# Three transformer blocks, mixture of experts at the end: the last two experts' results are summed on chip instead of in DRAM

## The chip, the cores and the metric

The kernel runs on one core of a Trainium2 chip, in one launch. The metric is the device time of a launch in microseconds (us). TensorE (PE) does the matmuls, VectorE (DVE), ScalarE (ACT) and GpSimd (POOL) the rest; SP and POOL issue the DMAs.

## The reference, cut to what matters

Three blocks follow each other on a sequence of 512 tokens of 1024 features. Only the end of the third is touched by the change:

```
x  = layer_norm(ALPHA * x + xa, ln2_g, ln2_b)
ff = hierarchical_moe(x, ...)          # each token goes to 2 of 32 experts
x  = layer_norm(ALPHA * x + ff, ln3_g, ln3_b)
```

An expert computes `(silu(x Wg) * (x Wu)) Wd`, with Wg and Wu of 1024 by 512 and Wd of 512 by 1024; a token's result is the sum of its two experts' outputs, each times a routing weight. The weights of one expert are 6.3 MB in float32. Products are made accurate by splitting each factor into a high and a low part (`H` and `L`) that TensorE takes in its one-pass float32 format (fp32r).

## The kernel before, in words

Routing sorts the 32 experts by the number of their tokens. Three experts come first by number ("fixed", `N_FIX`), so that their weights can be loaded before the routing is known; columns 18 to 31 (`N_BIG` on) hold the experts with the fewest tokens. Those are "small": at most 64 tokens, whose high and low parts stand side by side in the 128 columns of one operand, so that each step takes two matmuls instead of three; in exchange the two halves are added by 16 `fold` matmuls (L2137). A big expert takes 48 matmuls of 512 columns for gate and up and 24 for down; a small one 32 and 16.

The list `cols` (L2179) gives the order: five big experts, then small and big in turn, and a small one (column 31) as the last. The experts lie in a pipeline written out by hand: the block under `tc.manual_schedule` (L2203) fixes the order on PE, ACT, DVE, POOL and SP. In step `i` PE does the first half of the gate product of expert `i+1`, the transposes (or folds) of expert `i` (`mid`), the rest of the gate, `down` of `i`, and `up` of `i+1`; in step 30 `up` comes before `down`. The weights come in 12 pieces of 512 KB per expert, issued by SP (L1839); ACT casts each to its high part (L189) and DVE subtracts to get the low part (L190), up to five pieces ahead of PE, in five pairs of buffers.

`gather` (L2079) fetches an expert's tokens from `x2d`, the DRAM copy of the normalized residual that `resid_ln` spills at L415. `down` ends with two ACT evictions of PSUM times the routing weight (L2151) and an indirect DMA from POOL that adds the rows to `zd` in DRAM (L2152). `zd` has two halves of 512 rows; the second takes the low halves of small experts. Both are zeroed by eight DMAs (L1321) in the source of block 3, which depend on constants alone.

After the experts `K.x` (slot "X") is loaded from `x2d` (L2231). Then comes a loop over overflow experts (L2236) with a trip count read from the routing; in this trace its body does not run, but each engine reads the count, waits for the others' semaphores and for the DMA queues, and branches. Then eight DMAs from POOL add both halves of `zd` to the four tiles of `K.x` (L2255), two for a tile, and the last layer norm goes tile by tile: statistics on DVE for tile 0 and on ACT for the others, a power on POOL (L197), two DVE passes (L2266, L2267) and a store (L2268). Outside the manual block a planner places the instructions by its costs; so SP issues the zero fills at the kernel's start and the load of L2231 early in the expert stage.

Of the kernel before, what the change touches and what calls it, by code (L numbers as in the profile page):

```python
# [8 lines left out]
F32 = mybir.dt.float32  # L9
F32R = mybir.dt.float32r  # L10
I32 = mybir.dt.int32
AF = mybir.ActivationFunctionType
# [4 lines left out]
P = 128  # L17
S = 512
# [63 lines left out]
class K:  # L82
# [305 lines left out]
    def resid_ln(self, w, act, nk, xd, g, b, slots, zslot="A", spill=None, korder=None, after=None, mid=None):  # L388
        nc = self.nc
        g_, b_ = self.brow(g), self.brow(b)  # L390
        zt = self.slot(zslot, [P, 4, D])
        def reload():
            if xd is not None:
                for t in range(4):
                    nc.sync.dma_start(self.x[:, t], xd[t])
            if mid:
                mid[1]()

        if xd is not None:
            self.new_x()  # L400
        x = self.x
        hT = {}
        st = self.small([P, 4, 2, 6])

        def fn(half):
            def f(t, ps):
                hs = slice(half * 512, half * 512 + 512)
                nc.vector.scalar_tensor_tensor(zt[:, t, hs], x[:, t, hs], ALPHA, ps, ALU.mult, ALU.add)
                nc.vector.bn_stats(st[:, t, half], zt[:, t, hs])
                if half:  # L410
                    if not hT and slots:
                        hT[0] = self.hTn = self.new_hT(*slots)
                    self.layer_norm(x[:, t], zt[:, t], g_, b_, st[:, t])
                    if spill is not None:
                        nc.sync.dma_start(spill[t * P:(t + 1) * P], x[:, t])  # L415
                    if after:
                        after(t)
                    else:
                        self.to_hT(x[:, t], t, *hT[0], ps="t")
            return f  # L420

        for half in range(2):
            self.lin_b(w, half * 512, 512, act, fn(half), nk=nk, korder=korder, tail=3 * half,
                       mid=None if half else (mid[0] if mid else 0, reload))
# [881 lines left out]
def block3(K, out):  # L1306
# [10 lines left out]
    kd, vd = K.dram([P, 8, 256]), K.dram([P, 2, 512])  # L1317

    zd = K.dram([2 * S, D])
    for t in range(8):  # L1320
        nc.sync.dma_start(zd[t * P:(t + 1) * P].rearrange("p (a b) -> p a b", a=4),  # L1321
                          K.cst[:, C_CAUS - 384:C_CAUS - 128].unsqueeze(1).to_broadcast([P, 4, 256]))
    K.psum(f="f", nO="D", nS="B", nT="C", g="A")
# [552 lines left out]
        nc.tensor.transpose(ps[:, P:P + 36], lT[:, t % 2], K.ident[:36, :36])  # L1876
        tt(lg[:, t], ps[:, P:P + 36], bias, ALU.add)

    K.resid_ln(A("xa_wo"), K.actf((oH, oL)), 8, None, A("ln2_g"), A("ln2_b"), None, spill=x2d, after=logits)
    while K.bg:  # L1880
        K.bg.pop(0)()
    eslot = []
# [21 lines left out]
    with ExitStack() as ctx:  # L1904
# [166 lines left out]
        class Expert:  # L2071
            def __init__(self, i, c, small=False):
                self.i, self.small = i, small
                self.it, self.ws = (itok[:, c:c + 1], wsl[:, c:c + 1]) if isinstance(c, int) else c
                self.n = 64 if small else P

            def gather(self):
# [62 lines left out]
                tt(hT, sg, pt[:, 256:512], ALU.mult)  # L2140
                K.split(self.dH[:, :, 0:64], self.dH[:, :, 64:128], hT.rearrange("p (k t) -> p k t", k=4))

            def down(self, parts):
                yt = yt2[self.i % 2]
                pss = [K.psc() for _ in range(2)]
                for k in range(4):
                    h, l = parts()
                    for half, ps in enumerate(pss):
                        self.step(ps, self.dH, self.dL, k, 4, h[:, half], l[:, half])
                for half, ps in enumerate(pss):  # L2150
                    nc.scalar.activation(yt[:, half * 512:half * 512 + 512], ps, AF.Copy, scale=self.ws)  # L2151
                nc.gpsimd.indirect_dma_start(out=zd, out_offset=bass.IndirectOffsetOnAxis(ap=self.it, axis=0),  # L2152
                                             in_=yt, in_offset=None, bounds_check=2 * S - 1, oob_is_err=False, compute_op=ALU.add)


        class Feed:
# [10 lines left out]
        def ln3():  # L2167
            rows = brow(), brow()
            for dst, n in zip(rows, ("ln3_g", "ln3_b")):
                nc.sync.dma_start(dst[0:1], A(n).rearrange("(o d) -> o d", o=1))  # L2170
                for half in range(2):
                    hs = slice(half * 512, half * 512 + 512)
                    ps = K.psf()
                    mm(ps, K.cst[0:1, C_TRIU:C_TRIU + P], dst[0:1, hs], start=True, stop=True)
                    nc.scalar.copy(dst[:, hs], ps)
            return rows


        cols = [*range(N_FIX + 2), *(c for i in range(13) for c in (N_BIG + i, N_FIX + 2 + i)), 31]  # L2179

        def psrc(c):
            if c < N_FIX:
# [20 lines left out]
        with tc.manual_schedule(engines={getattr(mybir.EngineType, n) for n in ORDERED}):  # L2203
            for i in range(3):
                E[i].gather()
                if i < 2:
                    E[i].xT()
            E[0].gate1(feed)
            E[0].gate2(feed)
            E[0].up(feed)  # L2210
            for i, ex in enumerate(E):
                n1 = E[i + 1] if i < 31 else None
                if i == 8:
                    g_, b_ = ln3()
                if n1:
                    n1.gate1(feed)
                ex.mid()
                if n1:
                    n1.gate2(feed)
                if i < 30:  # L2220
                    E[i + 2].xT()
                if i < 29:
                    E[i + 3].gather()
                if i == 30:
                    n1.up(feed)
                ex.down(feed)
                if i < 30:
                    n1.up(feed)
        K.new_x()
        for t in range(4):  # L2230
            nc.sync.dma_start(K.x[:, t], x2d[t * P:(t + 1) * P])  # L2231

        it1 = rp.tile([P, 1], I32)
        ws1 = rp.tile([P, 1], F32)
        nx = nc.values_load(eidi[0:1, 7:8], min_val=0, max_val=7)
        with tc.For_i(0, nx, 1) as i:  # L2236
            ev = nc.values_load(eidi[0:1, bass.ds(i, 1)], min_val=0, max_val=31)
            nc.vector.tensor_copy(it1, itok[:, 32:39][:, bass.ds(i, 1)])
            nc.vector.tensor_copy(ws1, wsl[:, 32:39][:, bass.ds(i, 1)])
            src = [w[bass.ds(ev, 1)].rearrange("o r n -> (o r) n") for w in (wG, wU, wD)]  # L2240
            ex, parts = Expert(0, (it1, ws1)), Feed([lambda p=p: eload(p) for p in epieces(*src)])
            ex.gather()
            ex.xT()
            ex.gate1(parts)
            ex.gate2(parts)
            ex.up(parts)
            ex.mid()
            ex.down(parts)

        jt = K.slot("hH", [P, 4, D])  # L2250
        mu = rp.tile([P, 4, 4], F32)
        st = rp.tile([P, 2, 6], F32)
        for t in range(4):
            for z in (zd[t * P:(t + 1) * P], zd[S + t * P:S + (t + 1) * P]):
                nc.gpsimd.dma_start(K.x[:, t], z, accum_op=ALU.add)  # L2255
        for t in range(4):
            z, j, m_ = K.x[:, t], jt[:, t], mu[:, t]
            if t == 0:
# [51 lines left out]
```

## Time and profile before

| what | value |
|---|---|
| median of 3 runs | 2969.16 us (2954.52 to 2970.5) |
| profiled execution | 2949.98 us, of which 2.1 us lie outside its span |
| PE busy | 2815.3 us (95%) |
| DVE, ACT, POOL busy | 1731.2, 1391.1, 181.9 us |
| last expert matmul ends | 2901.9 us |
| end of the span | 2947.9 us |

All times from a view are counted from the span's start. A PE matmul's listed duration is longer than the distance to the next one, as matmuls are pipelined; the distance is its price. The mean number of bytes in flight says little: the expert stage (from about 2340 us) moves some 370 GB/s, the rest far less. A DMA's row on POOL or SP is its issue; the transfer itself ends later, at its landing.

### The profile page before, as it was taken

The page shows a single profiled execution, that of the slowest core. Times are in us where ns is not written, and L with a number is a line of the kernel's source. Part 1 is how long each engine was busy: PE and PEld are TensorE (multiplying, and loading weights), DVE is VectorE, ACT ScalarE, POOL GpSimd, SP SyncE. Part 2 cuts the span into 40 slices and gives each one's busy share as a digit, 9 for nine tenths or more (in the row PEclk, how much of TensorE's full clock was granted, in tenths as well). Part 3 has the DMA queues.
Part 4 walks back from the last instruction along what each step waited for, and adds up shares of the span by engine and source line. Part 5 has one row for each costly group of instructions (what it writes and reads, how often), then busy time and mean ns, then how long its engine had stood idle before and what let it go on. Part 6 is the DMA issues. An engine that isn't in the chain of part 4 may idle for free. (4 is left out here: it accounts for less than half of the span.)

```text
span 2947.9 us, 38804 instructions
## 1 busy us (share of the span) xinstructions
PE 2815.3 (95%) x14484; PEld 2339.1 (79%) x14484; DVE 1731.2 (59%) x2827; ACT 1391.1 (47%) x2325; POOL 181.9 (6%) x149
## 2 busy tenths in 40 slices
PE   8999999999999999999999999999999699999993
PEld 7788878888878878778888889787877588888882
DVE  4543453434576666755333362766564798998994
ACT  4432333332345445532222223756333388888883
POOL 0000000000000000000000000000000111221112
PEclk9999999999999989999999999999999799999996
DMA  6233333333331222133333344111432699999994
GB/s 205 86 93 93 100 93 95 98 99 94 119 86 47 68 61 58 47 121 100 95 100 93 100 137 124 36 37 56 164 121 108 217 351 384 381 375 377 384 376 89
DMA packets 332488, 432.76 MB, mean 147 GB/s; under 512 B 33583, under 2 KB 242154, under 8 KB 332298
## 3 DMA queue, kind: packets, MB, share of 16 engines
q1 hardware_dynamic: 322826, 417.52, 42.2%
q0 software_dynamic: 9472, 12.74, 2.0%
q8 instruction: 114, 1.87, 0.3%
q14 instruction: 76, 0.62, 0.1%
HBM read 419.04 MB, written 32.51 MB: 153 GB/s over the span
## 5 line engine op out<-in xcount | busy, mean ns | idle before, releaser
L164 DVE TENSOR_TENSOR wl<-raw,wh 128x1024 fp32r<-128x1024 f32 (+2 forms) x322 | 391.0, 1214 | 681.2 <-ACT wh L163 678.0
L163 ACT CAST wh<-raw 128x1024 fp32r<-128x1024 f32 (+2 forms) x322 | 336.4, 1045 | 862.2 <-PE pf L272 368.0
L272 PE MATMUL pf<-hL,wh 128*128 128x512 f32 x1272 | 502.0, 395 | 0.0
L272 PE MATMUL pf<-hH,wh 128*128 128x512 f32 x1208 | 477.9, 396 | 0.0
L272 PE MATMUL pf<-hH,wl 128*128 128x512 f32 x1208 | 475.8, 394 | 0.0
L272 PEld LDWEIGHTS pf<-hL,wh 128*128 128x128 f32 x1272 | 239.6, 188 | 50.5 <-issue 3.1
L272 PEld LDWEIGHTS pf<-hH,wh 128*128 128x128 f32 x1208 | 227.5, 188 | 52.5 <-issue 4.6
L272 PEld LDWEIGHTS pf<-hH,wl 128*128 128x128 f32 x1208 | 227.2, 188 | 48.7 <-issue 2.6
L190 DVE TENSOR_TENSOR wl<-ew,wh 128x1024 fp32r<-128x1024 f32 x186 | 216.9, 1218 | 6.2 <-ACT wh L189 5.5
L2098 PE MATMUL pc<-wh,hL 128*128 128x512 f32 x512 | 204.0, 398 | 0.0
L2099 PE MATMUL pc<-wl,hL 128*128 128x512 f32 x512 | 200.8, 392 | 0.0
L197 POOL TENSOR_TENSOR s<-s,mhalf 128x1 f32<-128x1 f32 (+1 forms) x69 | 57.9, 839 | 2234.4 <-DVE s L195 2228.8
L189 ACT CAST wh<-ew 128x1024 fp32r<-128x1024 f32 x186 | 184.4, 1056 | 8.4 <-PE pc L316 4.6
L347 PE MATMUL pf<-wh,hH 128*128 128x256 f32 (+2 forms) x576 | 163.9, 285 | 0.0
L314 PE MATMUL pc<-wh,B 128*128 128x512 f32 x416 | 163.1, 392 | 0.0
L315 PE MATMUL pc<-wl,B 128*128 128x512 f32 x416 | 162.8, 391 | 0.0
L348 PE MATMUL pf<-wl,hH 128*128 128x256 f32 (+2 forms) x576 | 162.6, 282 | 0.0
L349 PE MATMUL pf<-wh,hL 128*128 128x256 f32 (+2 forms) x576 | 162.0, 282 | 0.0
L316 PE MATMUL pc<-wh,C 128*128 128x512 f32 x320 | 124.6, 389 | 0.0
L2101 PE MATMUL pc<-wh,hL 128*128 128x512 f32 x288 | 113.7, 395 | 0.0
L2098 PEld LDWEIGHTS pc<-wh,hL 128*128 128x128 f32 x512 | 97.4, 190 | 19.9 <-issue 0.8
L2099 PEld LDWEIGHTS pc<-wl,hL 128*128 128x128 f32 x512 | 97.1, 190 | 19.5
(718 smaller groups left out, 5851.9 us busy)
## 6 DMA issues: line engine op xcount, KB each, us to landing
raw<-w_in SPq DMA_DIRECT2D x111, 512.0 KB, 4.0
raw<-w_ff SPq DMA_DIRECT2D x64, 512.0 KB, 3.9
ew<-moe_w_down SPq DMA_DIRECT2D x64, 512.0 KB, 12.5
B<-moe_w_gate SPq DMA_DIRECT2D x64, 512.0 KB, 7.2
hH<-moe_w_up SPq DMA_DIRECT2D x64, 512.0 KB, 11.4
A<-moe_w_down SPq DMA_DIRECT2D x64, 512.0 KB, 9.7
ew<-moe_w_up SPq DMA_DIRECT2D x62, 512.0 KB, 10.0
ew<-moe_w_gate SPq DMA_DIRECT2D x60, 512.0 KB, 10.3
```

The lines of the kernel that those rows point to most:

```text
L163: nc.scalar.copy(h, raw)
L164: nc.vector.tensor_sub(l, raw, h)
L189: self.nc.scalar.copy(h, src)
L190: self.nc.vector.tensor_sub(l, src, h)
L272: self.nc.tensor.matmul(ps[:n, sl], u[:, k], v[:, sl], start=(k == 0 and i == 0 and sl.start == 0), stop=(k == nk - 1 and i == 2), skip_gr ...
L314: mm(pss[t][:, :n], ah[:, ts], wh[:, k], start=(kg == 0), stop=False)
L315: mm(pss[t][:, :n], ah[:, ts], wl[:, k], start=False, stop=False)
L347: mm(o[t], ah[:, ts], wh[:, k], start=st, stop=False, skip_group_check=True)
L348: mm(o[t], ah[:, ts], wl[:, k], start=False, stop=False, skip_group_check=True)
L349: mm(o[t], al[:, ts], wh[:, k], start=False, stop=(kg == nk - 1), skip_group_check=True)
L2098: mm(ps, aH[:, k], h, start=(k == 0), stop=False)
L2099: mm(ps, aH[:, k], l, start=False, stop=(self.small and k == n - 1))
```

## The change: what it does, and the diff

The results of the last two experts in the list no longer go to DRAM. `down(keep=True)` splits them, times the routing weight, into a high part (ACT) and a low part (DVE), written into the expert's own, no longer needed, input buffers; and it builds four one-hot matrices per expert on DVE, slot against token of a tile, from the table of token numbers. `combine` multiplies them: for each tile and half 4 matmuls into a PSUM bank, and a DVE addition to `K.x`. To that end both last experts are big ones: `cols` starts with three big experts, alternates from there, and ends with two big ones.

The first half of `zd` starts as the residual (`resid_ln` spills each tile twice) instead of zeros, so four zero fills and the load of `x2d` at the end go. The eight loads of `zd`, four plain and four adding, are issued by POOL at the start of step 30, inside the manual order; an overflow expert, in the loop, goes by `combine` as well.

```diff
-                    if spill is not None:
-                        nc.sync.dma_start(spill[t * P:(t + 1) * P], x[:, t])
+                    for d in spill or ():
+                        nc.sync.dma_start(d[t * P:(t + 1) * P], x[:, t])
...
-    for t in range(8):
+    for t in range(4, 8):
...
-    K.resid_ln(..., spill=x2d, after=logits)
+    K.resid_ln(..., spill=(x2d, zd), after=logits)
...
+                if keep:
+                    self.yH, self.yL = (fl(v) for v in xh2[self.i % 2])
+                    self.oh = K.raw.tile([P, 4, P], F32R, name=K.nm("oh"), tag="raw")
+                    for t in range(4):
+                        ts_(self.oh[:, t], cc(G_I128, P), t * P + 1.0, self.tk, ALU.add, ALU.is_equal)
+                    for half, ps in enumerate(pss):
+                        hs = slice(half * 512, half * 512 + 512)
+                        nc.scalar.activation(self.yH[:, hs], ps, AF.Copy, scale=self.ws)
+                        stt(self.yL[:, hs], ps, self.ws, self.yH[:, hs], ALU.mult, ALU.subtract)
+                    return
...
+        def combine(*es):
+            for t in range(4):
+                for half in range(2):
+                    hs = slice(half * 512, half * 512 + 512)
+                    ps = K.psc()
+                    todo = [(e.oh[:, t], y[:, hs]) for e in es for y in (e.yH, e.yL)]
+                    for i, (o, y) in enumerate(todo):
+                        mm(ps, o, y, start=(i == 0), stop=(i == len(todo) - 1))
+                    tt(K.x[:, t, hs], K.x[:, t, hs], ps, ALU.add)
...
-        cols = [*range(N_FIX + 2), *(c for i in range(13) for c in (N_BIG + i, N_FIX + 2 + i)), 31]
+        cols = [*range(N_FIX), *(c for i in range(14) for c in (N_BIG + i, N_FIX + i)), N_BIG - 1]
...
+                if i == 30:
+                    K.new_x()
+                    for z in (0, S):
+                        for t in range(4):
+                            nc.gpsimd.dma_start(K.x[:, t], zd[z + t * P:z + (t + 1) * P],
+                                                **({"accum_op": ALU.add} if z else {}))
...
-                ex.down(feed)
+                ex.down(feed, i > 29)
...
-        K.new_x()
-        for t in range(4):
-            nc.sync.dma_start(K.x[:, t], x2d[t * P:(t + 1) * P])
+            combine(E[30], E[31])
...
-            ex.down(parts)
+            ex.down(parts, True)
+            combine(ex)
...
-        for t in range(4):
-            for z in (zd[t * P:(t + 1) * P], zd[S + t * P:S + (t + 1) * P]):
-                nc.gpsimd.dma_start(K.x[:, t], z, accum_op=ALU.add)
```

## Rows read from the trace of the kernel before

**Rows 1.** The page's first line: span and instructions.
```profile
span 2947.9 us, 38804 instructions
```

**Rows 2.** Chain that ended last, its longest piece: start us, us, what.
```profile
2919.26 11.03 DMA X<-dr
```

**Rows 3.** Timeline 2880 to 2950: start, us, engine line op, [idle before <-releaser].
```profile
2890.88 3.81 PEld L2137 LDWEIGHTS pt<-fold,scr 128*128 128x128 f32 x16
...
2896.65 0.80 PE L2098 MATMUL pc<-wh,dHL 128*128 128x512 f32 x1 [1.82 <-DVE dHL L190]
...
2901.31 0.40 PE L2098 MATMUL pc<-wh,dHL 128*128 128x512 f32 x1
...
2901.51 1.27 ACT L2151 ACTIVATE C<-pc,wsl 128x512 f32<-128x512 f32 x2 [5.37 <-PE pc L2099]
2901.54 0.40 PE L2099 MATMUL pc<-wl,dHL 128*128 128x512 f32 x1
2903.05 1.56 POOL L2152 DMA_INDIRECT dr<-C,itok  x1 [7.96 <-ACTq L2236]
2907.76 2.75 POOL L2255 DMA_DIRECT2D X<-dr  x3 [3.16 <-issue]
...
2922.58 1.28 DVE L2260 BATCH_NORM_STATS2 st<-X 128x6 f32<-128x512 f32 x2 [25.98 <-DMA X<-dr]
...
2927.26 15.52 SPq L2268 DMA_DIRECT2D out<-X  x4
...
2929.64 1.28 DVE L2267 SCALAR_TENSOR_TENSOR X<-X,s,bc 128x1024 f32<-128x1024 f32 x1 [0.44 <-POOL s L197]
...
2932.64 1.28 DVE L2267 SCALAR_TENSOR_TENSOR X<-X,s,bc 128x1024 f32<-128x1024 f32 x1 [0.46 <-POOL s L197]
2936.90 1.06 ACT L2263 ACTIVATE hH<-X 128x1024 f32<-128x1024 f32 x1 [6.62 <-DMA X<-dr]
```

**Rows 4.** Windows of 20 us: length, busy us PE PEld DVE ACT POOL, clock, DMA.
```profile
2820.00:2840.00 20.00, 20.00 (x93) 17.30 (x93) 17.09 (x19) 16.62 (x24) 4.51 (x3) 1.00 0.97 368
```

**Rows 5.** Waits 2320 to 2900: us in total, times, longest.
```profile
PEld pc L2099 <- DVE wl L190: 0.2, 1, 0.2
```

**Rows 6.** Timeline of DVE, single instructions of the routing and the expert stage.
```profile
2310.91 0.29 DVE L1951 TENSOR_TENSOR C<-C,mv 128x128 f32<-128x128 f32 x1
...
2374.72 0.68 DVE L2124 TENSOR_TENSOR scr<-scr,pc 128x512 f32<-128x512 f32 x1
...
2392.49 0.68 DVE L2124 TENSOR_TENSOR scr<-scr,pc 128x512 f32<-128x512 f32 x1
...
2844.40 0.68 DVE L2124 TENSOR_TENSOR scr<-scr,pc 128x512 f32<-128x512 f32 x1
...
2878.76 0.68 DVE L2124 TENSOR_TENSOR scr<-scr,pc 128x512 f32<-128x512 f32 x1
...
2889.03 4.62 DVE L190 TENSOR_TENSOR wl<-A,wh 128x1024 fp32r<-128x1024 f32 x4
```

**Rows 7.** Windows of 1 us in the last expert's down product, columns as above.
```profile
2898.00:2899.00 1.00, 1.00 (x4) 0.71 (x4) 0.00 (x0) 0.00 (x0) 0.00 (x0) 0.50 0.00 0
```

**Rows 8.** Timeline of POOL: the scatter of the third last expert.
```profile
2873.52 1.83 POOL L2152 DMA_INDIRECT dr<-C,itok  x1 [16.11 <-ACT C L2151]
```

**Rows 9.** The scatters' line L2152: durations of the issue in ns, landing.
```profile
L2152 POOL DMA_INDIRECT dr<-C,itok x32: 1553/1848/2343, 2370.0 to 2903.0; - x32
...
DMA to landing us min/median/max: 2.7/8.2/10.9
```

**Rows 10.** DMA issues 2840 to 2950: count, size, median us to landing.
```profile
X<-dr POOLq DMA_DIRECT2D x8, 512.0 KB, 9.0
```

**Rows 11.** Timeline of SP: zero fills, the reload of X, the last weights.
```profile
32.12 9.63 SPq L1321 DMA_DIRECT2D dr<-cst  x8
...
2374.83 1.80 SPq L2231 DMA_DIRECT2D X<-dr  x4
...
2864.97 4.08 SPq L1839 DMA_DIRECT2D A<-moe_w_down  x4
```

More of the change, by code (lines that the diff above doesn't have):

```diff
@@ L1877, in logits @@
         tt(lg[:, t], ps[:, P:P + 36], bias, ALU.add)
-    K.resid_ln(A("xa_wo"), K.actf((oH, oL)), 8, None, A("ln2_g"), A("ln2_b"), None, spill=x2d, after=logits)
+    K.resid_ln(A("xa_wo"), K.actf((oH, oL)), 8, None, A("ln2_g"), A("ln2_b"), None, spill=(x2d, zd), after=logits)
     while K.bg:
@@ L2073, in __init__ @@
                 self.i, self.small = i, small
-                self.it, self.ws = (itok[:, c:c + 1], wsl[:, c:c + 1]) if isinstance(c, int) else c
+                self.it, self.ws, self.tk = [v[:, c:c + 1] for v in (itok, wsl, tab)] if isinstance(c, int) else c
                 self.n = 64 if small else P
@@ L2141, in mid, with down @@
                 K.split(self.dH[:, :, 0:64], self.dH[:, :, 64:128], hT.rearrange("p (k t) -> p k t", k=4))
-            def down(self, parts):
+            def down(self, parts, keep=False):
                 yt = yt2[self.i % 2]
@@ L2225, in block3 @@
                     n1.up(feed)
-                ex.down(feed)
+                ex.down(feed, i > 29)
                 if i < 30:
                     n1.up(feed)
-        K.new_x()
-        for t in range(4):
-            nc.sync.dma_start(K.x[:, t], x2d[t * P:(t + 1) * P])
+            combine(E[30], E[31])
         it1 = rp.tile([P, 1], I32)
         ws1 = rp.tile([P, 1], F32)
+        tk1 = rp.tile([P, 1], F32)
         nx = nc.values_load(eidi[0:1, 7:8], min_val=0, max_val=7)
@@ L2239, in block3 @@
             nc.vector.tensor_copy(ws1, wsl[:, 32:39][:, bass.ds(i, 1)])
+            nc.vector.tensor_copy(tk1, tab[:, 32:39][:, bass.ds(i, 1)])
             src = [w[bass.ds(ev, 1)].rearrange("o r n -> (o r) n") for w in (wG, wU, wD)]
-            ex, parts = Expert(0, (it1, ws1)), Feed([lambda p=p: eload(p) for p in epieces(*src)])
+            ex, parts = Expert(0, (it1, ws1, tk1)), Feed([lambda p=p: eload(p) for p in epieces(*src)])
             ex.gather()
```

## The prediction

> **What bounds the kernel now.** I read the page first: the profiled span is 2947.9 us [rows 1]; the whole execution, 2949.98, is 2.1 more, and the median of the runs shown, 2969.16, lies 19.2 above it. Then the chain that ended last: its largest piece is not an engine but a transfer, X<-dr, with a link of 11.03 us [rows 2]. The timeline of the last 70 us shows why. The last expert matmul starts at 2901.54 and lasts 0.40, so PE is done at 2901.94, 46.0 us before the end. In these 46 us come the scatter (2903.05), the loop's code, eight loads (from 2907.76), and a layer norm that starts at 2922.58 and waits for loads between its tiles: the last tile gets going at 2936.90, and the last store is issued at 2927.26 + 15.52 = 2942.78 [rows 3].
>
> Before that the expert stage is PE's: 20.00 of 20 us busy at full clock, while the DMA engines are busy 0.97 of the time at 368 GB/s [rows 4]. Both are nearly full, but the weights are in time: all that PE waited for them is 0.2 us [rows 5]. So what is taken from DMA there gains nothing in this trace, and what is taken from PE gains all.
>
> **The change part by part.**
>
> *The order of experts.* Place 3 gets a small expert for a big one, place 31 a big one for a small one; the 30 others stay. A big expert lasts 17.8 us (2374.72 to 2392.49), a pair 34.4 (2844.40 to 2878.76), so a small one 16.6 [rows 6]. Place 3 thus takes 1.2 us off everything behind it. Place 31 needs 48 matmuls for gate and up instead of 32; at a distance of 0.23 us (2901.31 to 2901.54) that adds 16 x 0.23 = 3.7 [rows 3].
>
> *The end of the last expert.* Before, it runs from the folds' start at 2890.88 to 2901.94, 11.1 us, with an idle gap of 1.82 before `down` [rows 3]; after that gap the granted clock in 2898 to 2899 is 0.50, the lower level of 1.2 GHz [rows 7]. Now there are no folds, but DVE is late: behind the last weight split stand four one-hot compares of 128x128 at 0.29 each (nearest row, same size, another operation), two low parts at 0.68 from PSUM, and only then the low part of the new `hd` at 0.68 [rows 6]. That last split goes into a buffer that PE frees six matmuls before the end of `down` of place 30 (1.4 us); a subtraction takes 4.62 / 4 = 1.2 [rows 6], the cast before it about as much (estimate from that), so it ends 1.0 behind `down`. 1.0 + 1.2 + 1.4 + 0.7 = 4.3 us. PE can use 0.45 of that for two matmuls. From there 22 matmuls take 22 x 0.23 = 5.1, and about 1.2 more if the clock falls after the wait, as it did before; together 10.2, in place of 11.1. Bounds: 8 us if DVE interleaves the compares, 13 if all 24 run at half clock. PE's end: 2901.94 - 1.2 + 3.7 - 0.9 = 2903.5.
>
> *The combine.* 32 matmuls of 512 columns in fp32r, the form of L2098. For the first bank place 30's two run at once; place 31's last low part comes 1.6 us after PE's end (two ACT evictions at 0.64, two DVE ones at 0.68 behind the first [rows 3, 6]), and then six banks of 4 x 0.23 follow: 1.9 + 5.5 = 7.4. DVE adds each bank in 0.68, less than the 0.92 that PE takes for one, so only the last shows: 8.2 us. Bounds: 7.9, and 15 if PE stays at the lower level. The waits are short, so I take 8.2.
>
> *The loads of zd.* Eight issues on POOL behind the scatter of place 29. POOL has nothing else to do then but the loop's code, and the powers of the layer norm. That scatter is issued at 2873.52 [rows 8], now 1.2 earlier, and lands after 8.2 (2.7 to 10.9) [rows 9]: 2880.5. The eight lasted 2936.90 - 2907.76 = 29.1 us before, with adding loads that wait for their tile's first one, 9.0 each in the median [rows 3, 10]; the same now gives 2909.6. The four plain ones now go first and side by side, so I take 25: 2905.5. The last tile's additions are due at 2903.5 + 6.7 = 2910.2. Hidden, with 0.6 to 5 us to spare; each microsecond beyond costs one. The last weights are issued at 2864.97 to 2869 [rows 11], so these loads do not push them back.
>
> By the Trainium skill (SBUF — State Buffer, "SBUF: two separate sides") a DMA from POOL can stand still while VectorE holds the port that both share, since POOL writes the descriptors; its box speaks of a DMA that waits until the VectorE operation's end. Here DVE splits weights all the time, and the scatters' issues take 1.85 us in the median and at most 2.34, against 1.56 at 2903.05 with DVE idle [rows 3, 9]: a delay of 0.3 to 0.8, not a split's whole 1.22. By the rule in full, 8 x 1.2 = 9.6 us would move the landing to 2915 and cost 5; by the rows, 8 x 0.3 = 2.4 stays hidden.
>
> *The loop.* It now stands between the additions and the layer norm. Before, POOL needed 3.16 us from its last issue's end to its first load, with its code, its waits and a first fetch behind the branch [rows 3]; that is the nearest row for DVE. I take 3.1 (1 to 5). What used to hide it is gone: the other engines were waiting for loads.
>
> *The layer norm.* The same instructions, but all tiles are there at once: tile 0 takes 2922.58 to 2927.26 = 4.7 from statistics to store, a further tile 3.0 (2929.64 to 2932.64) [rows 3], together 13.7. ACT's statistics run ahead, as they wait for no load. 11.9 if the planner fills DVE's wait for the power with the next tile. From the end of the last store's issue, 2942.78, to the span's end it was 5.1; with the issue itself, some 0.35, 5.5, and that stays.
>
> *What goes or moves at no price.* The reload of X ran on SP at 2374.83 [rows 11], in the stage where PE had its weights: hidden, 0. Four of eight zero fills, 1.2 us of SP's queue each at 32 to 41 us [rows 11], while PE has work: 0 (to -2). The four extra spills follow one of the same tile on the same queue; at worst they push the preloads of the first experts' weights back by 2 MB at 368 GB/s = 5.7 us [rows 4]; PE did not wait for weights, so 0, or 2 if the first gather gets in behind them.
>
> **Sum.** PE ends at 2903.5; + 8.2 + 3.1 + 13.7 + 5.5 = 2934.0, against 2947.9: 13.9 us less, 2936 in place of 2949.98. Applied to the median, 2969.16 - 13.9 = 2955.3. Of the 46.0 us behind PE's end 30.5 stay, and 1.6 of the gain is paid back by the big expert in last place.
>
> **The rivals.**
>
> *The loads are late.* They land behind 2910, at 29 us or more and slow issues, or PE stays at half clock in the combine (7 us). For it: the margin is 0.6 at the upper bound, and the landing of the scatter alone varies by 8. Against: eight were served in 29 with the layer norm's waits between them. Price 5 to 9, so 2962.
>
> *They do not overlap at all (slower).* If something holds POOL's loads until place 31 is done (a wait on slot X, on `zd`, or behind the loop's preparations), they start at 2903.5 and end 29 later, at 2932.6, where the layer norm no longer runs between them: + 1.4 for the last additions + 3.1 + 13.7 + 5.5 = 2956.3, 8 more than before; with four adding loads one after the other (11 + 4 x 9.0 = 47) it is 2974, 26 more. The middle is +17, 2986. It decides from a landing after 2924. For it: before, the adding loads waited for the plain ones. Against: slot X is free early, as the reload of before was issued into it at 2374.83 [rows 11].
>
> *More than the tail.* The runs 20 us above the profiled execution may be such in which weights come late. There the missing 2 MB reload, 5.7 us at 368 GB/s [rows 4], would count, and DVE's filled waits add 1.8: 21 less, 2948. Against: nothing here shows such a run.
>
> **How the numbers follow.** Runs of this kernel tell some 0.5%, 14.8 us, from no change, and the forecast is just short of it. Chances: forecast 0.64, split by its own bounds into 0.31 beyond 14.8 us and 0.33 within; late loads 0.14, within; no overlap 0.10, of it 0.08 slower; more than the tail 0.12, faster. Faster 0.43, same 0.49, slower 0.08. The range: the terms' bounds are -6 and +9, and the runs of one kernel spread by 16 to 20, with the profiled execution at the bottom: down to 2932 (2936 and some), up to 2967 (late loads and a little more).
>
> **What would show it.** Right: PE's last expert matmul at 2901 to 2906; a combine of some 8 us with PE at clock 1.00; the last X<-dr landing before its tile's addition; DVE's first statistics about 3 us behind the last addition; tiles 3.0 apart. The chain would name PE and DVE, not X<-dr. Wrong: an addition that waits for DMA, a PE wait for weights in the expert stage, a clock of 0.50 through the combine, or a join that takes over 5 us because each engine fetches code behind the branch.

## The result, and the profile after

The changed kernel takes 2942.95 us in the median of 20 runs (2933.41 to 2963.12), the kernel before 2963.27 over 20 runs beside them (2951.92 to 2970.52). The ratio is 0.9944, 95% interval 0.9928 to 0.9961: 16.6 us less, 11.6 to 21.3 (the two medians differ by 20.3). One execution of the kernel before, beside the last runs below, took 5023 us at a clock of 0.729; it counts in no ratio and no median. The forecast was 2955.3, 13.9 less than the median of the three runs known then.

The two profiled spans hide this at first: 2947.9 us before [rows 1], 2946.2 after. The first row that tells why is the first expert's gate and up, long before anything the change touches. Timeline of DVE, the first such eviction, before and then after:

```profile
2357.68 0.68 DVE L2124 TENSOR_TENSOR scr<-scr,pc 128x512 f32<-128x512 f32 x1
```

```profile
2371.65 0.68 DVE L2124 TENSOR_TENSOR scr<-scr,pc 128x512 f32<-128x512 f32 x1
```

The profiled execution after is 14.0 us late already. Windows (length, busy us of PE, PEld, DVE, ACT, POOL, granted clock, DMA) of the second block of the network, before:

```profile
1150.00:1170.00 20.00, 18.46 (x137) 16.09 (x137) 10.01 (x22) 11.26 (x25) 0.00 (x0) 1.00 0.32 93
1170.00:1183.00 13.00, 12.54 (x78) 10.06 (x77) 10.52 (x32) 8.13 (x20) 0.00 (x0) 1.00 0.00 1
1250.00:1272.00 22.00, 20.13 (x124) 15.98 (x123) 17.92 (x54) 16.57 (x49) 3.15 (x5) 1.00 0.00 1
```

and after:

```profile
1150.00:1170.00 20.00, 18.45 (x134) 15.78 (x133) 10.14 (x22) 11.39 (x25) 0.00 (x0) 0.98 0.32 93
1170.00:1183.00 13.00, 13.00 (x48) 10.22 (x48) 6.71 (x21) 6.81 (x17) 0.00 (x0) 0.51 0.00 1
1250.00:1272.00 22.00, 21.76 (x80) 16.80 (x79) 13.47 (x38) 12.47 (x30) 0.00 (x0) 0.53 0.03 13
```

PE was just as busy ahead of it (18.46 and 18.45 of 20 us), and then it runs at the lower level, 1.2 GHz, in one execution and not in the other: 48 matmuls instead of 78 in the same 13 us. That is chance between executions, not the change: in another execution of the changed kernel (e0_again below) the same eviction starts at 2362.57. Every span below is therefore cut in three: up to that first eviction, from there to the end of the last expert's last matmul ("the expert stage"), and the tail behind it. Before: 2357.68, 544.3, 46.0. After: 2371.65, 545.5, 29.1. The change is in the last two numbers: +1.2 and -16.9, together -15.7.

The tail after. PE (timeline: start us, us, engine line op, [idle before <-releaser]); the second last row is the last matmul of `down(31)`:

```profile
2907.70 0.39 PE L2101 MATMUL pc<-wh,dHL 128*128 128x512 f32 x1
2907.94 0.63 PE L213 MATMUL pt<-cst,scr 128*128 128x128 f32 x4
2909.84 0.40 PE L2099 MATMUL pc<-wl,dHL 128*128 128x512 f32 x1
2911.84 0.50 PE L2101 MATMUL pc<-wh,dHL 128*128 128x512 f32 x1 [1.60 <-DVE dHL L190]
...
2916.74 0.39 PE L2101 MATMUL pc<-wh,dHL 128*128 128x512 f32 x1
...
2918.01 6.87 PE L2174 MATMUL pc<-hL,oh 128*128 128x512 f32 x29 [0.20 <-DVE hL L2159]
```

DVE in the same stretch:

```profile
2904.16 4.92 DVE L190 TENSOR_TENSOR wl<-A,wh 128x1024 fp32r<-128x1024 f32 x4
2909.00 0.87 DVE L2155 TENSOR_SCALAR oh<-cr,tab 128x128 fp32r<-128x128 f32 x4
2909.78 1.40 DVE L2159 SCALAR_TENSOR_TENSOR hL<-pc,wsl,hL 128x512 fp32r<-128x512 f32 x2
2911.10 0.68 DVE L190 TENSOR_TENSOR dHL<-pt,dHL 128x512 fp32r<-128x512 f32 x1
...
2918.55 0.69 DVE L2175 TENSOR_TENSOR X<-X,pc 128x512 f32<-128x512 f32 x1
...
2924.92 0.69 DVE L2175 TENSOR_TENSOR X<-X,pc 128x512 f32<-128x512 f32 x1 [0.22 <-PE pc L2174]
2928.36 1.29 DVE L2286 BATCH_NORM_STATS2 st<-X 128x6 f32<-128x512 f32 x2 [2.75 <-ACT hH L2289]
```

POOL and SP:

```profile
2887.73 1.94 POOL L2163 DMA_INDIRECT dr<-C,itok  x1 [16.50 <-ACT C L2162]
2894.63 2.24 POOL L2241 DMA_DIRECT2D X<-dr  x4 [4.96 <-DVE scr L2124]
...
2904.02 0.85 POOL L2241 DMA_DIRECT2D X<-dr  x1 [0.57 <-DMA X<-dr]
...
2938.07 1.52 POOL L197 TENSOR_TENSOR s<-s,mhalf 128x1 f32<-128x1 f32 x1 [2.13 <-DVE s L195]
```

```profile
2933.05 8.22 SPq L2294 DMA_DIRECT2D out<-X  x4
```

The eight loads are issued from 2894.63 to 2904.02 while DVE still splits weights. The instructions of their line have these landings:

```profile
DMA to landing us min/median/max: 3.6/7.6/10.7
```

The longest is that of the load at 2904.02: 2914.7, 20.1 us behind the first issue and 2.4 ahead of PE's end. What the first load waited for is the scatter issued at 2887.73: it lands at 2894.05, 0.58 ahead of that issue; in every kernel here whose loads follow a scatter the distance is 0.57 to 0.58. No addition waits for DMA: each of the last seven waits 0.2 us for PE. The layer norm's 26.0 us for X<-dr [rows 3] have become 2.75 for the loop's entry. The chain that ended last, shares of the stretch from 2820 to the end by engine and line, names no transfer any more, in place of [rows 2] (the profile follows it back to 2926.3, so PE does not stand in it either):

```profile
by line: POOL s L197 3.4%; issue 2.3%; DVE X L2293 2.0%; POOLq L2332 1.2%; DVE st L2286 1.0%; ACT hH L2289 0.9%; ACTq L2263 0.2%; DVE s L195 0.2%; DVE mu L2287 0.2%; DVEq L2263 0.0%
```

### The profile page after: what moved, and what is told of

The parts are those of the page before. It is cut to its first block, busy times and chain, and to the rows that moved or that the text cites. A ratio compares the mean times of both kernels' runs of the same rounds, so it can differ in the third digit from the quotient of the medians.

```text
span 2946.2 us, 38882 instructions
## 1 busy us (share of the span) xinstructions
PE 2838.2 (96%) x14516; PEld 2357.2 (80%) x14516; DVE 1741.5 (59%) x2847; ACT 1389.8 (47%) x2325; POOL 177.8 (6%) x147
## 6 DMA issues: line engine op xcount, KB each, us to landing
B<-moe_w_gate SPq DMA_DIRECT2D x64, 512.0 KB, 10.2
```

## The experiments

Theory: the gain is the tail, because the loads of `zd` run under the last two experts. Rival: it is made elsewhere (order of experts, the reload and zero fills that went, or chance). A second question came from the tail that is left: what ends it.

| kernel | runs | median us | ratio to before | at clock 0.980 | expert stage | of it at half clock | tail |
|---|---|---|---|---|---|---|---|
| before | 31 | 2959.81 | 1 | 2948.1 | 544.3 | 6.8 | 46.0 |
| changed | 20 | 2942.95 | 0.9944 (0.9928 to 0.9961) | 2942.5 | 545.5 | 6.8 | 29.1 |
| e0_again | 10 | 2943.93 | 0.9956 (0.9935 to 0.9977) | 2942.4 | 548.7 | 13.7 | 29.1 |
| e1_order | 10 | 2960.55 | 1.0003 (0.9979 to 1.0027) | 2947.9 | 547.1 | 13.7 | 46.9 |
| e2_late | 10 | 2957.61 | 1.0004 (0.9980 to 1.0028) | 2950.0 | 545.5 | 6.8 | 43.1 |
| e3_keep1 | 10 | 2949.17 | 0.9980 (0.9960 to 0.9999) | 2946.1 | 547.0 | 13.7 | 39.8 |
| e4_no_loop | 8 | 2942.08 | 0.9926 (0.9902 to 0.9951) | 2940.2 | 548.6 | 13.7 | 24.7 |
| e5_defer | 9 | 2947.73 | 0.9942 (0.9919 to 0.9966) | 2940.7 | 545.6 | 10.2 | 29.1 |
| e6_ln_first | 6 | 2938.16 | 0.9919 (0.9891 to 0.9948) | 2943.1 | 545.4 | 6.8 | 29.4 |
| e7_both | 12 | 2944.08 | 0.9942 (0.9921 to 0.9964) | 2941.3 | 543.7 | 6.8 | 29.4 |
| e9_no_pool | 6 | 2939.15 | 0.9925 (0.9899 to 0.9951) | 2939.7 | 547.2 | 13.7 | 26.8 |
| e10_pool_last | 1 | 2943.67 | - | 2943.7 | 548.9 | 13.7 | 30.7 |

A ratio is to runs of the kernel before made beside those of its row, and not the quotient of the medians shown: for the changed kernel they are the 20 of the section above, for e0 to e3 the 31 of the first row, for e4 to e7 22 others (median 2962.77), for e9 10 (2965.3). Stage and tail are of the one profiled execution, read as above. "Of it at half clock" are the us of the stage for which the granted clock is 0.50, from the trace's record of the clock: two executions of the changed kernel differ by 6.8 of these us and by 3.2 in the stage (545.5 and 548.7), so stages are compared at equal half clock, at 0.47 us for each. Before and changed have 6.8 each, so +1.2 is at equal half clock; but in the kernel before half of the 6.8 lies in the last `down` ([rows 7]), in the changed kernel all of it ahead of that.

"At clock 0.980": each run lists its mean granted clock, and in the changed kernel's 20 runs time follows it, from 2963.12 us at 0.972 to 2933.41 at 0.983, by 2.66 us per 0.001 (a fitted line, with 1 us of scatter; the other kernels' own fits give 2.1 to 2.5). Brought to one clock, the runs of a kernel scatter by 1 to 2 us (standard deviation) and lie within 4 to 8 us of each other, instead of 13 to 30. One execution of the kernel before does not follow the line: 2956.70 us at 0.930. The mean also counts the idle tail, in which the clock stands at 0.50, so a short tail looks 0.45 us per us worse than it is: between before and changed that is 22 us at 0.50 (41 against 19, by the windows of the last 60 us), 10 us, and 2948.1 - 2942.5 + 10 = 15.6 us, the same as by the profile. (With the fit of the kernel before itself, 2.18, its figure is 2950.0 and the tail's share 8: 15.5.)

**The changed kernel again.**

> The changed kernel once more, to see what of its time is chance. Theory of the tail: whatever the span comes to, from the start of the last expert matmul to the span's end it is 29.5 us again (+-0.5; 46.4 in the kernel before), and where the span differs from the first profile's 2946.2, PE has lost or won the difference in stretches at a granted clock of 0.50 long before the experts (windows of 100 us from 1000 to 1400). Rival, the gain is made elsewhere: the tail itself varies by several us from run to run, or the clock stretches stand in the expert stage.

The tail is 29.12 again (29.11 in the first), span 2940.4. The expert stage was 3.2 us longer, with clocks of 0.97 and 0.98 in three of its windows of 100 us, so such stretches are not only in the second block. The tail itself does not vary.

**The order of experts alone**, in the kernel before:

```diff
-cols = [*range(N_FIX + 2), *(c for i in range(13) for c in (N_BIG + i, N_FIX + 2 + i)), 31]
+cols = [*range(N_FIX), *(c for i in range(14) for c in (N_BIG + i, N_FIX + i)), N_BIG - 1]
```

> The kernel before with nothing but the changed kernel's order of experts. Theory of the tail: the order gains nothing; place 3 gives 1.2, place 31 takes 3.7, the folds of the last expert go (-0.9), so +1.6 us against the kernel before, and the tail behind PE's last expert matmul stays at 46.0 with the loads of X in it. Rival, the gain is made elsewhere (here: the order): 5 to 16 us less than before.

Ratio 1.0003, the tail 46.9: the order gains nothing. Nor does it cost the 1.6 us that was expected: at equal half clock the stage is 0.4 us shorter than before (547.1 - 3.2 = 543.9 against 544.3), and at one clock the time is the same (2947.9 and 2948.1). The 1.6 held a -0.9 for the end of the last expert in which PE also waits for the one-hots and low parts of place 30, and this kernel has none: from the end of `down(30)` to PE's end it takes 7.4 us, against 9.0 in the changed kernel and 11.1 before (from the folds' start). By that the changed kernel's stage is longer than this one's, 1.6 at equal half clock.

**The loads held behind the last expert**, all else as changed:

```diff
-                if i == 30:
-                    K.new_x()
-                    for z in (0, S):
-                        ... (the eight loads)
+            K.new_x()
+            nc.gpsimd.tensor_copy(gate, E[31].yL[:, D - 1:D])
+            for z in (0, S):
+                ... (the eight loads)
             combine(E[30], E[31])
```

> The changed kernel with its eight loads held on POOL until the last expert's last low part is there (a copy of one column of it stands ahead of them), so that nothing of them lies beside the experts. Theory of the tail: the first load is issued about 2 us behind PE's end, the last lands some 20 to 23 us later, the last additions wait for it, then join, layer norm and last store as in the changed kernel: 44 to 46 us from PE's end to the span's end instead of 29.1, so 15 to 17 us slower than the changed kernel, level with the kernel before (-2 to +2). The prediction's rival had +8 to +26 over the kernel before for this. Rival, the gain is made elsewhere: still 10 us or more faster than before, as the order, the missing reload and the missing zero fills are all still there.

PE ends at 2899.93. Timeline of POOL, then of DVE:

```profile
2902.17 2.24 POOL L2256 DMA_DIRECT2D X<-dr  x4 [0.48 <-issue]
...
2911.73 0.84 POOL L2256 DMA_DIRECT2D X<-dr  x1 [0.74 <-DMA X<-dr]
```

```profile
2913.98 1.28 DVE L2175 TENSOR_TENSOR X<-X,pc 128x512 f32<-128x512 f32 x2 [12.54 <-DMA X<-dr]
...
2921.61 1.28 DVE L2175 TENSOR_TENSOR X<-X,pc 128x512 f32<-128x512 f32 x2 [0.65 <-DMA X<-dr]
2925.11 1.29 DVE L2287 BATCH_NORM_STATS2 st<-X 128x6 f32<-128x512 f32 x2 [2.22 <-ACT hH L2290]
```

The first addition waits 12.54 us for its tile, the last is done 23.0 us behind PE's end instead of 8.5, the tail is 43.1 (1 less than expected), and the time is that of before, ratio 1.0004. So the whole gain hangs on when the loads run; one-hot product, order, missing reload and missing fills together bring none. It also bounds the prediction's slower rival: without any overlap the change would have been level, not +8 to +26, since the eight loads took 19.3 us and not 29 or 47.

**Only the last expert kept on chip**; place 30 is scattered, and the loads follow its scatter:

```diff
-                if i == 30:
+                if i == 31:
                     K.new_x()
-                ex.down(feed, i > 29)
+                ex.down(feed, i > 30)
-            combine(E[30], E[31])
+            combine(E[31])
```

> Only the last expert's result stays on chip; place 30 is scattered to DRAM again, and the eight loads stand behind that scatter. Theory of the tail: it is the distance between the last scatter and PE's end that hides the loads. Place 30's scatter is issued about 9 us ahead of PE's end and lands about at it or just behind, the loads then take 20 us: the last lands 11 to 15 us behind the point where its addition is due, so 10 to 15 us slower than the changed kernel, of its 17 us of tail only 2 to 6 are left. Rival, keeping any result on chip is what gains: as fast as the changed kernel or 1 to 2 us faster (two products of a bank fewer, 3.7 us).

```profile
2898.93 1.55 POOL L2163 DMA_INDIRECT dr<-C,itok  x1 [19.58 <-ACT C L2162]
2904.19 2.23 POOL L2241 DMA_DIRECT2D X<-dr  x4 [3.71 <-issue]
```

```profile
2916.01 1.28 DVE L2175 TENSOR_TENSOR X<-X,pc 128x512 f32<-128x512 f32 x2 [9.30 <-DMA X<-dr]
```

PE ends at 2905.2, the loads begin 1.0 ahead of it, and the tail is 39.8: 10.7 longer than with two experts kept, 6.2 shorter than before. The scatter was issued 6.3 us ahead of PE's end, not 9, and landed at 2903.62, 0.6 ahead of the first load. What counts is the distance between the last scatter's landing and PE's end; a second expert kept buys it. (The stage is 1.7 shorter here at equal half clock, as place 30's parts are missing, so in all it is 9 us slower than with two, a little less than was expected.)

**No loop** (this leaves out the overflowing experts, of which these inputs have none):

```diff
-        nx = nc.values_load(eidi[0:1, 7:8], min_val=0, max_val=7)
-        with tc.For_i(0, nx, 1) as i:
-            ...
```

> The changed kernel without its loop over overflowing experts (with these inputs it runs no time around, so only its entry is left out). Theory: the 2.76 us between the last addition and the first statistics are the entry's price alone; they go, ACT's statistics of the later tiles can begin while PE still combines, and from PE's end to the span's end it is 24 to 26.4 instead of 29.1, ratio to before 0.9935 to 0.9947 where the changed kernel has 0.9944 to 0.9956. Rival: DVE's statistics wait for something else (the last addition's write, code not fetched yet), and less than 1 us goes.

```profile
2911.39 0.69 DVE L2175 TENSOR_TENSOR X<-X,pc 128x512 f32<-128x512 f32 x1 [0.24 <-PE pc L2174]
2911.99 0.69 DVE L2266 BATCH_NORM_STATS2 st<-X 128x6 f32<-128x512 f32 x1
2912.60 1.30 DVE L2175 TENSOR_TENSOR X<-X,pc 128x512 f32<-128x512 f32 x2
```

24.65 behind PE's end, 4.5 less: the entry costs its 2.75, and the other 1.7 go with statistics that now slip in between the additions, as the rows show.

**Place 30's parts moved behind place 31's split:**

```diff
                 if i == 30:
                     n1.up(feed)
+                if i == 31:
+                    E[30].hold()          # one-hots, high and low parts, out of down()
                 ex.down(feed, i > 29)
+            E[31].hold()
             combine(E[30], E[31])
```

> The changed kernel with place 30's one-hots, high and low parts moved on ACT and DVE behind place 31's product and split, so that place 31's low part no longer stands behind them. Theory: PE's wait ahead of place 31's down product (3.74 us) is DVE's lateness, 4 compares and 2 low parts of it; it shrinks to 1.5 to 2, PE's end comes 2 us sooner (read as the distance between the last matmul of place 30's down and that of place 31's), the combine's own length stays at 8.5 or grows by less than 1, as the moved work lies beside the down product. Rival: DVE is the bound there; the work comes later and the combine waits for it, so that down and combine together last as long as before (within 0.5 us).

```profile
2895.53 0.39 PE L2101 MATMUL pc<-wh,dHL 128*128 128x512 f32 x1
2895.76 0.63 PE L213 MATMUL pt<-cst,scr 128*128 128x128 f32 x4
2897.07 0.50 PE L2098 MATMUL pc<-wh,dHL 128*128 128x512 f32 x1 [0.68 <-ACT dHL L189]
2897.41 0.40 PE L2099 MATMUL pc<-wl,dHL 128*128 128x512 f32 x1
2897.79 0.50 PE L2101 MATMUL pc<-wh,dHL 128*128 128x512 f32 x1
```

From the end of `down(30)` to the first matmul that needs the low part it is now 2897.79 - 2895.92 = 1.9 instead of 2911.84 - 2908.09 = 3.75; the last matmul of `down(31)` comes 1.9 us sooner behind the last of `down(30)` (2902.69 - 2895.53 = 7.16 against 9.04), and the combine's length stays at 8.48. At one clock, 2940.7 against 2942.5: the same 1.8, though at an uncertainty of about 0.8 the timing alone would not carry it.

**The layer norm ahead of the loop** (into another slot, and repeated in the loop's body):

```diff
+        last_ln()
         it1 = rp.tile([P, 1], I32)
         ...
             combine(ex)
+            last_ln()
```

> The changed kernel with the last layer norm and its stores ahead of the loop, from X into another slot; the loop's body repeats them after its own combine, so the result is the same with any inputs. Theory: the loop's entry (2.76 us) then stands behind the layer norm, beside the 5.3 us in which the last store lands, and costs little: 24 to 27 us from PE's end to the span's end instead of 29.1. Rival: the entry waits until the stores have landed, and its price is paid behind them: 28 to 30.

```profile
2918.99 6.52 SPq L2277 DMA_DIRECT2D out<-B  x4
L2339 POOLq DRAIN  x3: 46/103/5785, 2928.6 to 2935.0; - x3
```

The rival was right: 29.4. Layer norm and additions now run into each other, and the last store is issued 19.4 us behind PE's end instead of 23.8 (at 2918.99 + 6.52 - 0.33 = 2925.18); but from there to the end it is 10.05 us instead of 5.3, and all is given back. The trace shows where they go. The store lands at 2928.23, 3.05 us behind its issue; SP passes its last wait of the loop's entry at 2928.26, and POOL branches at 2928.50. The second row is what POOL's queue closes with, an instruction named DRAIN (three of them; durations in ns, min/median/max): the long one starts at 2928.6, lasts 5.79, and the end follows 0.83 behind it. At one clock it is 0.6 slower than the changed kernel. The low ratio, 0.9919, is six executions with few stretches at half clock.

**Both edits together.**

> The two edits together (place 30's parts behind place 31's split, layer norm ahead of the loop), which compute all that the changed kernel does. Theory: they add up, 2 us before PE's end and 2 to 5 behind it, so 4 to 7 us less than the changed kernel and a ratio to before of 0.992 to 0.994. Rival: either is given back (the combine waits for DVE, the entry waits for the stores): 0 to 2 us less.

Stage 543.7, which is 1.8 less than the changed kernel's, and tail 29.4, which is not less: one edit is kept, the other given back, as its rival had it.

**No power on POOL.** In e6 the last store landed 7 us ahead of the end, so there a store's landing is not what ends the program. In the changed kernel POOL's last power ends at 2939.59, 6.65 us ahead of the end:

```diff
-            rs = K.rstd(m_[:, 1:2], 1, 1.0 / D if t else 1.0, 1e-5 / ALPHA ** 2)
+            vs, rs = K.small([P, 1]), K.small([P, 1])
+            ts_(vs, m_[:, 1:2], 1.0 / D if t else 1.0, 1e-5 / ALPHA ** 2, ALU.mult, ALU.add)
+            nc.scalar.activation(vs, vs, AF.Sqrt)
+            nc.vector.reciprocal(rs, vs)
```

> The kernel with place 30's parts moved (the edit of the run before that shortened PE's wait), and in the last layer norm the power -0.5 taken off POOL: a square root on ACT and a reciprocal on DVE give the same factor. So POOL has no work after the loop's entry. In the kernel before, the changed kernel and the one without a loop, POOL's last power ends 6.82, 6.65 and 6.63 us ahead of the span's end, and the last store is issued 5.47, 5.30 and 5.28 ahead of it; with the layer norm ahead of the loop the last store was issued 10.05 ahead. Theory: what sets the end is POOL, which needs some 6.6 us to close behind its last work, and not the landing of the last store; with POOL idle from the entry on, the last store's issue to the end falls to 3 to 4 us, and with the layer norm 0 to 1 us shorter, PE's end to the span's end is 26 to 27.5 instead of 29.1. Rival: the end is the store's landing; 5.3 us stay, 28 to 29.1 in all.

```profile
core 0 of [0], span 2930.4 us
...
2925.52 1.29 DVE L2303 SCALAR_TENSOR_TENSOR X<-X,s,bc 128x1024 f32<-128x1024 f32 x1
...
2919.15 8.01 SPq L2304 DMA_DIRECT2D out<-X  x4
...
L2342 POOLq DRAIN  x3: 50/103/5785, 2913.5 to 2930.1; - x3
```

The last store's issue begins at 2919.15 + 8.01 - 0.33 = 2926.83, and the end follows 3.6 us later instead of 5.3; the layer norm, from the first statistics to that issue, takes 12.0 instead of 12.6 although the first square root loads a table for 1.28. POOL's DRAIN still takes 5.79, but from 2913.5 on, behind the loop's entry and beside the layer norm. The tail is 26.8.

**One more instruction on POOL**, behind the layer norm:

```diff
             nc.sync.dma_start(out[t * P:(t + 1) * P], z)
+        late = rp.tile([P, 1], F32)
+        nc.gpsimd.tensor_copy(late, K.x[:, 3, D - 1:D])
```

> The changed kernel with one copy of a column on POOL behind the last layer norm (it reads the last tile's result, and nothing reads what it writes). It ends some 1.6 us later than POOL's last power does now. Theory that POOL's closing sets the end: the span's end moves with it, 1.5 to 1.9 us later, 30.6 to 31 us from PE's end, and 6.8 to 7.2 from the last store's issue. Rival, the last store's landing sets it: 29.1 and 5.3 as before.

```profile
core 0 of [0], span 2941.8 us
...
2934.94 0.18 POOL L2296 COPY late<-X 128x1 f32<-128x1 f32 x1 [1.39 <-DVE X L2293]
...
L2334 POOLq DRAIN  x3: 50/109/6017, 2934.9 to 2941.5; - x3
```

```profile
2927.01 8.22 SPq L2294 DMA_DIRECT2D out<-X  x4
```

The copy ends at 2935.12, the program 6.65 later, as in the changed kernel; the tail is 30.7 (PE ends at 2911.09), 1.6 longer, with the layer norm and its stores as they were. With that the end is POOL's: its DRAIN is over at 2934.91 + 6.02 = 2940.93, 5.81 behind the copy, and the end comes 0.84 later. In the changed kernel the same DRAIN is over 5.81 behind the last power:

```profile
L2332 POOLq DRAIN  x3: 50/109/7368, 2938.0 to 2946.0; - x3
```

This is one execution of that kernel; it is read within its trace.

The version with place 30's parts moved and no power on POOL has the shortest tail of the complete kernels, 26.8, and the moved parts' 1.9 us ahead of PE's end besides. At one clock it takes 2939.7 against 2942.5 of the changed kernel, and 1 us more is hidden there, as its idle tail is shorter: 3.8 us, against 2.3 + 1.9 = 4.2 by the traces. Its ratio to before is 0.9925 (0.9899 to 0.9951); from the changed kernel's the timing alone cannot part it.

## Why the prediction held, point by point

- *What bounds the kernel.* Right: the tail was transfers, and that is what went. With the same edits but the loads late, nothing is left of the gain.
- *The end of the last expert.* PE's wait was forecast as 4.3 us, DVE being late with a split, four compares, two low parts and the low part of `hd`. It was 3.75, with just these in just this order (2904.16 to 2911.78 on DVE). Not seen was the fall of the clock to the lower level behind the wait, as in [rows 7], for which 1.2 us stood in the sum: matmuls are 0.23 apart right from 2912.17. From the end of place 30's `down` to PE's end it is 9.0 us, forecast 10.2 (11.1 before). Ahead of that, at equal half clock, the stage is 1.7 longer, here as in the kernel with the order alone; forecast 2.5 (-1.2 + 3.7). So both terms were too high, by 1.2 and 0.8, and that the stage came out 1.2 longer, forecast 1.6, is luck: 1.6 of it is half clock ahead of the last `down`, of which the changed kernel's execution has more.
- *The combine.* 8.5 behind PE's end, forecast 8.2, paced by PE as said: DVE waits 0.22 before each later addition.
- *The loads.* Forecast 25 us from the first issue to the last landing, measured 20.1, and 19.3 in the kernel with late loads (PE's end + 2.2 to PE's end + 21.6). What was too long was the 29.1 us that it started from: there all eight loads add, and the last was issued only at 2930.58. Of four plain and four adding ones in one go each adding one still takes 7.8 to 10.7 us ([rows 10] has 9.0), but several are under way at a time, and they land 2.5 to 3.6 us apart. What weights beside them would cost is not shown: in the changed kernel the last weights have landed before the first load is issued (from 2891 to 2894 the DMA engines move 21 GB/s), and in the windows below both kernels move the same. The spare time was 9.3 us (last landing 2914.7, last tile's addition 2924.02), not 0.6 to 5.
- *DVE in POOL's way.* The eight issues of the changed kernel lie in a stretch where DVE is busy for 10.77 of 10.90 us, those of the kernel with late loads in one where it is busy for none of 11. Windows, then the line of the loads (duration of an issue in ns, min/median/max), the changed kernel first:

```profile
2894.00:2904.90 10.90, 10.90 (x51) 9.07 (x51) 10.77 (x11) 8.98 (x10) 5.70 (x8) 1.00 0.79 230
...
L2241 POOL DMA_DIRECT2D X<-dr x8: 537/725/894, 2894.6 to 2904.0; - x8
```

```profile
2901.60:2912.60 11.00, 2.46 (x11) 1.69 (x9) 0.00 (x0) 0.00 (x0) 5.79 (x9) 0.72 0.81 232
...
L2256 POOL DMA_DIRECT2D X<-dr x8: 537/724/892, 2902.2 to 2911.7; - x8
```

The issues take the same. The Trainium skill (SBUF — State Buffer, "SBUF: two separate sides") has a POOL DMA's descriptors wait while VectorE runs an operation in a mode that takes two ports, and its example is a copy. The splits here are subtractions of two inputs, and for them the trace shows no such delay. The prediction read the page more widely, as of any VectorE operation; neither its 9.6 us nor the 2.4 that it took from the scatters' issues is there.
- *The loop.* 2.75, forecast 3.1. Taking the loop out brings 4.5, as it also keeps the layer norm from reaching into the combine, which the prediction did not see.
- *The layer norm.* 12.6 to the last store's issue, forecast 13.7: DVE waits for the power at the first and the last tile (0.46 and 0.44 us) and not at the two between, which run into each other; so 1.1 of the lower bound's 1.8 us came.
- *The end.* Forecast 5.5 behind the last store, measured 5.3, but this step was right for a wrong reason. It took the store for what ends the program. POOL ends it, and the number only stayed, by luck, because the last power ends 1.35 us ahead of the last store's issue in both kernels.
- *No price for the rest.* Reload, zero fills and spills: the kernel with late loads has them all changed and is level with before, within the 7 us of its interval. The traces say it more sharply: of three executions with 71.7 us at half clock ahead of the first expert's eviction, that eviction starts at 2357.68 in the kernel before, and at 2358.21 and 2356.43 with the change (e3_keep1, e9_no_pool).

So the tail is 29.1 where 30.5 was forecast, and the whole is -15.7 by the profile, -13.9 by the sum. Which side of its 14.8 us the gain lies on, the interval of 11.6 to 21.3 leaves open. The time itself was missed by 12.4 us, and most of that is no step of the sum: the median of before over 20 runs is 2963.27, 5.9 below the three runs that it was taken from; 1.8 is the sum's; and 4.6 is by how much the two medians of 20 differ more than the two traces (20.3 against 15.7), chance of the clock. Those stretches of half clock move single executions by up to 30 us, and three runs do not average them out. The two rivals on transfers, late loads and no overlap, were wrong by 9.3 us of spare time; the third, that slow executions are ones whose weights come late, was wrong as well: they are ones in which the clock fell.

## What to carry to other kernels

A transfer at the end is worth hiding when its sources are complete early, and what makes them complete early is to keep the last producers' results out of DRAM: count how long the loads need (20 us here) and keep as many results as cover it (two experts; one left 10.7 us uncovered). Behind the last engine's work look for what really ends the program, by moving one instruction on each engine: here it was not the last store but POOL's last small power. Before spans of two kernels are compared, line up an instruction ahead of the change; here 14 of the 16 us of gain were hidden by clock in a part that is the same in both.

## What the runs showed of the hardware

- The granted clock falls to 0.50 in some executions and not in others, in the same code with the same 18.45 us of PE work in the 20 us ahead; time follows the mean clock by 2.66 us per 0.001 in the changed kernel, and that accounts for nearly all of the 30 us between its executions. What starts such a stretch is open; no experiment here was made on it.
- From the end of POOL's last instruction to the end of the program it is 6.82, 6.65, 6.63 and 6.65 us in four kernels (before, changed, no loop, one more instruction on POOL). Of that 5.8 to 6.0 are the DRAIN that POOL's queue closes with and 0.8 what follows it. With POOL idle from the loop's entry on, DRAIN runs beside the layer norm, and the last store's issue is 3.6 us ahead of the end. What DRAIN does in its 5.8 us, and whether it would be as long in a program whose POOL issues no DMA, was not tried.
- With a loop that runs no time around, 2.2 to 2.75 us pass between the last addition and the next work on DVE (without it the tail is 4.5 shorter), and behind the stores it costs as much or more: with the layer norm ahead of it, the store's 5.3 us to the end became 10.05. There the entry waits until the last store has landed (3.05 us behind its issue), 0.4 go until POOL is past the branch, and DRAIN with its 5.79 and the 0.83 to the end follow.
